# Two products on half of the rows each for the scores of a chunk's two heads, in place of one product padded with zeros

## The chip, the cores and the metric

The kernel runs on one core of a Trainium2 chip. A core has five engines that run side by side: TensorE (PE in the profile, with its weight loads as PEld), VectorE (DVE), ScalarE (ACT), GpSimd (POOL) and SyncE (SP, which issues DMAs). TensorE reads from the on-chip memory and writes to eight banks of accumulators (PSUM), 128 partitions by 512 float32 numbers each. The metric is the device time of one execution, in microseconds (us); less is better.

## The reference, cut to what matters

The program is a chain of three layers on 256 tokens of width 1024. The change is in the last mixer, in its recurrent branch: two directions (forward and backward), 16 heads of width 64, over 256 context tokens and then 256 tokens of the sequence. The recurrence is

```
def wkv_scan(s0, scan_in):
    def step(s, inp):
        w, kk, a, k, v, r = inp
        sa = jnp.einsum('dbhij,dbhj->dbhi', s, kk)
        s = s * w[..., None, :] - sa[..., :, None] * (kk * a)[..., None, :] + v[..., :, None] * k[..., None, :]
        return s, jnp.einsum('dbhij,dbhj->dbhi', s, r)
    return lax.scan(step, s0, scan_in)
```

The kernel computes it in chunks of 64 steps: eight chunks in each direction, four of the context and four of the sequence. Within a chunk it needs, for each head, the products of every step's vectors `kk*a` and `k` (scaled by decays) with every step's `kk` and, in the sequence's chunks, with every step's `r`, over the 64 channels of the head, masked to the steps that come before. These are the scores that the change is about.

## The kernel before, in words

The last mixer goes over eight pairs of heads (`i` from 0 to 7). For each pair there are four pieces of work: `rw_scores` (projections, decays, scores), `rw_inverse` (the inverse of a triangular matrix per chunk), `rw_chain` (the eight chunks one after the other) and `diff_head` (one head of the other branch, an attention). In one turn of the loop stand `chain(i)`, `inverse(i + 1)`, `heads(i + 1)` and `scores(i + 2)`, so four pairs are in work at a time. The order of the instructions on each engine is not the order of the code: the framework simulates the program when it is built and puts on each engine next what it takes to be ready. Each engine then works strictly through its own list.

A pair of heads takes 128 partitions: channels of the first head in partitions 0 to 63 and of the second in 64 to 127. In `rw_scores`, per direction `d`, `BK[:, c]` (L1682, L1685) holds for chunk `c` the 64 columns of `kk*a` and the 64 of `k` of both heads. `ap` (tiles `AL`, one of them in the space of `xT`) holds `kk` of the eight chunks and `r` of the last four, in a layout with an extra axis `o` for the head: L1679 and L1680 write head `o` on its own 64 partitions only, and the other 64 partitions of that column block are zeros, set once. So a product of `BK[:, c]` (128 weight columns) with `ap[:, c]` (128 columns: `o` by 64 steps) over all 128 partitions gives the scores of the two heads apart, in 128 rows.

The scores come in three tiles `mc` of PSUM per direction: at L1689 four products of 128 columns for the context's chunks; at L1696, twice, two products of 256 columns (`kk` and `r`) for two of the sequence's chunks each. VectorE multiplies them by a mask into `MA` and `MR`: L1690 once, L1699 four times. Then `BK` is transposed (L1703, tile `bt`). All of `rw_scores` (projections and `lo`, `la`, `kn`, `mc`, `bt`, `bo`, `gu`) draws its PSUM tiles from a pool of two banks, `a`, in turn (`self.banks(c2, a=2, i=1, r=2, d=2, k=1)`). `rw_chain` reads `MA` (L1743) and the zero-padded `AL` (L1747); `rw_inverse` reads `MA` (L1810 and on).

A float32 matmul stands in the trace as two passes, each a weight load and a matmul, so four products are eight rows there. Each row of the trace names the part of the array that it uses before the shape of the operand, as rows*columns: `128*128` is all of it, `64*128` one half of the rows.

Of the kernel before, what the change touches and what calls it, by code (L numbers as in the profile page):

```python
# [249 lines left out]
class K:  # L250
# [1351 lines left out]
    def rw_scores(self, i, h2):  # L1602

        nc, A = self.nc, self.A
        v_ = nc.vector
        g_ = nc.gpsimd
        p, tp = self.rp, self.rt
        lora = p.tile([128, 3, 128], F32, tag="lora", name=f"lora{i}", bufs=1)
        nc.sync.dma_start(lora, A["lora"][i])

        def proj(name, j, n):
            out = p.tile([128, n // T, T], F32, tag=name, name=f"{name}{i}", bufs=2 if name == "v" else 1)
            ps = self.psum(name, "k")
            self.wT(ps[:, :n], self.w2(24 + j), h2 if n > T else h2[:, :, T:])
            self.shift(ps[:, :n].rearrange("p (s t) -> p s t", t=T), j, out)
            return out

        lw = self.lw.rearrange("p s t -> p (s t)")
        c0 = math.exp(-0.5)

        def decays(d):

            pw, pa = self.psum("lo"), self.psum("la")
            nc.tensor.matmul(pw, lora[0:64, d], lw[0:64], start=True, stop=True)
            nc.tensor.matmul(pa, lora[64:128, d], lw[64:128], start=True, stop=True)
            t = tp.tile([128, 7, T], F32, tag="el", name=f"el{i}_{d}", bufs=1)
            sg, a, Pi = (t[:, 2 * m:2 * m + 2].rearrange("p s t -> p (s t)") for m in range(3))
            E3 = t[:, 6]
            nc.scalar.activation(sg, pw, AF.Tanh, bias=self.hb[:, 8 * d + i:8 * d + i + 1], scale=0.5)
            nc.scalar.activation(a, pa, AF.Tanh, bias=self.hb[:, 16 + 8 * d + i:17 + 8 * d + i], scale=0.5)  # L1630
            v_.tensor_scalar(t[:, 0:4], t[:, 0:4], 0.5, 0.5, op0=OP.mult, op1=OP.add)
            if d == 0:
                v_.tensor_tensor_scan(Pi, self.smask, sg, 0.0, op0=OP.mult, op1=OP.add)
            else:
                v_.tensor_tensor_scan(Pi[:, ::-1], self.smask, sg[:, ::-1], 0.0, op0=OP.mult, op1=OP.add)
            v_.tensor_sub(sg, Pi, sg)
            nc.scalar.activation(sg, sg, AF.Exp, scale=-c0)
            nc.scalar.activation(E3, Pi[:, T:], AF.Exp, scale=-c0)
            ends = Pi.rearrange("p (s c t) -> p s c t", s=2, t=64)
            nc.scalar.activation(WC[:, d].rearrange("p (s c) -> p s c", s=2), ends[:, :, ::-1, 0] if d else ends[:, :, :, 63], AF.Exp, scale=-c0)  # L1640
            nc.scalar.activation(Pi, Pi, AF.Exp, scale=c0)
            return sg, a, Pi, E3

        k = proj("k", 8 + i, 512)
        r = proj("r", i, T)

        kk = p.tile([128, 2, T], F32, tag="kk", name=f"kk{i}")
        sq = tp.tile([128, 2, T], F32, tag="sq", name=f"ksq{i}", bufs=1)
        v_.tensor_scalar(kk, k, self.pvec("rw_k_k", i), None, op0=OP.mult)
        nc.scalar.activation(sq, kk, AF.Square)  # L1650
        ps = self.psum("kn")
        nc.tensor.matmul(ps, self.bd, sq.rearrange("p j t -> p (j t)"), start=True, stop=True)
        rs = self.rstd(ps, 512, eps=self.lneps[:, 1:2])
        v_.tensor_mul(kk, kk, rs.rearrange("p (j t) -> p j t", j=2))

        AL = self.apart[i % 2]
        MA = p.tile([128, 2, 2, 8, 64], F32, tag="MA", name=f"MA{i}", bufs=2)
        MR = p.tile([128, 2, 2, 4, 64], F32, tag="MR", name=f"MR{i}", bufs=2)
        BKt = p.tile([128, 2, 7, 128], F32, tag="BKt", name=f"BKt{i}", bufs=2)
        WC = p.tile([128, 2, 8], F32, tag="WC", name=f"WC{i}", bufs=2)  # L1660
        for d in range(2):
            n = f"{i}_{d}"
            E1, a, E2, E3 = decays(d)
            t1 = E1

            def fl(x, s=None):
                x = x.rearrange("p (s t) -> p s t", t=T) if len(x.shape) == 2 else x
                if d:
                    x = x[:, :, ::-1]
                if s is None:  # L1670
                    return x.rearrange("p s (c t) -> p s c t", t=64)
                return x[:, s].rearrange("p (c t) -> p c t", t=64)

            BK = tp.tile([128, 8, 2, 64], F32, tag="BK", name="BK" + n, bufs=1)
            BK5 = BK.rearrange("p (s c) a t -> p s c a t", s=2)
            ap = AL[d]
            for o in range(2):
                rr = slice(64 * o, 64 * o + 64)
                v_.tensor_mul(ap[rr, :8, o].rearrange("p (s c) t -> p s c t", s=2), fl(kk)[rr], fl(E1)[rr])  # L1679
                v_.tensor_mul(ap[rr, 8:, o], fl(r, 0)[rr], fl(E3[:, None], 0)[rr])  # L1680
            v_.tensor_mul(t1, kk.rearrange("p s t -> p (s t)"), a)
            v_.tensor_mul(BK5[:, :, :, 0], fl(t1), fl(E2))  # L1682
            v_.tensor_scalar(a, a, self.pvec("rw_k_a", i), self.ka1[:, i:i + 1], op0=OP.mult, op1=OP.add)
            v_.tensor_mul(a, a, k.rearrange("p s t -> p (s t)"))
            v_.tensor_mul(BK5[:, :, ::-1, 1] if d else BK5[:, :, :, 1], *(x.rearrange("p (s c t) -> p s c t", s=2, t=64) for x in (a, E2)))  # L1685

            ps = self.psum("mc")
            for c in range(4):
                nc.tensor.matmul(ps[:, 128 * c:128 * c + 128], BK[:, c].rearrange("p a t -> p (a t)"), ap[:, c].rearrange("p o t -> p (o t)"), start=True, stop=True)  # L1689
            v_.tensor_mul(MA[:, d, :, 0:4].rearrange("p o c t -> p c o t"), ps.rearrange("p (c o t) -> p c o t", c=4, o=2),  # L1690
                          self.wmask[:, d, None, None, 0:64].to_broadcast([128, 4, 2, 64]))
            zz = ap.rearrange("p (m c) o t -> p m c (o t)", m=3)
            for c2 in range(2):
                ps = self.psum("mc")
                for c in range(2):
                    nc.tensor.matmul(ps[:, 256 * c:256 * c + 256], BK[:, 4 + 2 * c2 + c].rearrange("p a t -> p (a t)"), zz[:, 1:3, 2 * c2 + c], start=True, stop=True)  # L1696
                pv = ps.rearrange("p (c m o t) -> p m c o t", c=2, m=2, o=2)
                for m, dst in enumerate((MA[:, d, :, 4 + 2 * c2:6 + 2 * c2], MR[:, d, :, 2 * c2:2 * c2 + 2])):
                    v_.tensor_mul(dst.rearrange("p o c t -> p c o t"), pv[:, m], self.wmask[:, d, None, None, 64 * m:64 * m + 64].to_broadcast([128, 2, 2, 64]))  # L1699
            for s in range(2):  # L1700
                ps = self.psum("bt")
                for c in range(4 - s):
                    nc.tensor.transpose(ps[:, 128 * c:128 * c + 128], BK[:, 4 * s + c].rearrange("p a s -> p (a s)"), self.ident)  # L1703
                nc.scalar.copy(BKt[:, d, 4 * s:4 * s + 4 - s], ps.rearrange("p (c t) -> p c t", c=4)[:, :4 - s])
        v = proj("v", 16 + i, 512)

        sq = tp.tile([128, 2, T], F32, tag="sq", name=f"bsq{i}", bufs=1)
        v_.scalar_tensor_tensor(sq[:, 0], r[:, 0], self.pvec("r_k", i), k[:, 1], op0=OP.mult, op1=OP.mult)
        ps = self.psum("bo")
        nc.tensor.matmul(ps[:, :T], self.bd, sq[:, 0], start=True, stop=True)  # L1710
        bg = p.tile([128, 2, T], F32, tag="bg", name=f"bg{i}", bufs=2)
        v_.tensor_mul(bg[:, 0], v[:, 1], ps[:, :T])
        ps = self.psum("gu")
        nc.tensor.matmul(ps[:, :T], lora[:, 2], self.sgd[:, 0], start=True, stop=True)
        nc.scalar.copy(bg[:, 1], ps[:, :T])
        return v, AL, MA, MR, BKt, WC, bg
# [523 lines left out]
```

## Time and profile before

| | |
|---|---|
| median of 3 runs | 3490.37 us (3477.37 to 3495.87) |
| profiled execution | 3489.14 us |
| its span, first to last instruction | 3487.4 us |
| TensorE busy over the span | 92% |
| VectorE busy over the span | 66% |
| mean granted TensorE clock | 0.936 of full |
| stretch that holds all the scores of the mixer | 1600 to 2440 us of the span |

A busy TensorE is not TensorE at its peak: matmuls follow each other before the one ahead has ended, so the price of one in a row of equals is the distance from start to start, not its duration. The granted clock is given as a share of 2.4 GHz: it stands at 1.2 or at 2.4 GHz, and a number between is a mean over a stretch.

### The profile page before, as it was taken

What the parts mean: (1) busy time and instruction counts of PE and PEld (TensorE: products, weight loads), DVE (VectorE), ACT (ScalarE), POOL (GpSimd) and SP (SyncE); (2) the same over time, 40 slices, a digit from 0 to 9 for tenths busy, and PEclk for the clock granted to TensorE, in tenths of its full rate; (3) what the DMA queues carried; (4) which work ended last, traced back from release to release, by engine and by line L of the source; (5) the groups of instructions that cost most, each with busy time, mean ns of one, the idle gap of its engine ahead of it and who ended that gap; (6) DMA issues with size and microseconds to landing.
All of it is one profiled execution on the core that took longest, in us unless ns stands there. A gap on an engine that the chain in (4) does not pass through costs nothing. (4 is left out here: it accounts for less than half of the span.)

```text
span 3487.4 us, 67773 instructions
## 1 busy us (share of the span) xinstructions
PE 3207.4 (92%) x26800; PEld 2648.6 (76%) x26800; DVE 2309.6 (66%) x4717; ACT 1710.9 (49%) x3107; POOL 467.2 (13%) x478
## 2 busy tenths in 40 slices
PE   6989979989999999978899999899879989999999
PEld 4869967766668888746677677667779989988888
DVE  3568858753449999746766666566357767756665
ACT  4445423442226666514544544454436658755554
POOL 0000232200000000010000000000208853410000
PEclk8999988889999999988989888889789999999999
DMA  7666574478798999962111111111435545566775
GB/s 291 237 225 229 200 255 147 125 282 319 321 372 327 337 338 339 356 264 78 45 31 45 45 45 40 45 44 47 141 123 191 159 141 173 176 197 202 231 228 163
DMA packets 162435, 658.51 MB, mean 189 GB/s; under 512 B 18216, under 2 KB 37304, under 8 KB 118208
## 3 DMA queue, kind: packets, MB, share of 16 engines
q1 hardware_dynamic: 145344, 572.33, 46.6%
q0 software_dynamic: 16768, 81.80, 6.9%
q8 instruction: 212, 3.47, 0.4%
q14 instruction: 111, 0.91, 0.1%
HBM read 634.26 MB, written 19.79 MB: 188 GB/s over the span
## 5 line engine op out<-in xcount | busy, mean ns | idle before, releaser
L428 PE MATMUL mg<-mg,xs 128*64 128x256 f32 x1408 | 185.0, 386 | 3.7 <-ACT xf L1101 3.7
L1248 ACT ACTIVATE msg<-mg 128x128 f32<-128x128 f32 (+1 forms) x154 | 42.1, 273 | 260.3 <-PE mg L428 191.2
L428 PEld LDWEIGHTS mg<-mg,xs 128*64 128x64 f32 x1408 | 106.2, 138 | 68.1 <-issue 15.8
L331 PE MATMUL mod<-wm,c 128*32 128x256 f32 x1152 | 100.2, 452 | 50.0 <-DMA wm<-mods 45.5
L1363 POOL DMA_DIRECT2D h2h<-hch x1 | 1.0, 960 | 821.6 <-DVE squares L1372 821.6
L331 PEld LDWEIGHTS mod<-wm,c 128*32 128x32 f32 x1152 | 37.7, 123 | 87.7 <-DMA wm<-mods 44.4
L1814 POOL MEMSET X<- 128x272 f32 x8 | 3.0, 378 | 753.6 <-DVE UV L1754 217.9
L1249 DVE TENSOR_TENSOR msg<-msg,mg 128x128 f32<-128x128 f32 (+1 forms) x154 | 43.4, 282 | 76.4 <-ACT msg L1248 75.9
L328 POOL DMA_DIRECT2D wm<-mods x64 | 34.6, 541 | 386.2 <-PE mod L331 374.5
L2024 POOL TENSOR_SCALAR oh<-iota,idx 128x128 f32<-128x128 f32 x44 | 58.3, 1324 | 146.1 <-PE G L2034 146.1
L2027 ACT ACTIVATE oh<-oh,idx 128x128 f32<-128x128 f32 x212 | 69.1, 393 | 6.4 <-DVE oh L2019 6.4
L2019 DVE TENSOR_TENSOR oh<-iota,idx 128x1024 f32<-128x1024 f32 x53 | 67.6, 1278 | 0.0
L2034 PE MATMUL G<-oh 128*128 128x128 f32 x512 | 62.5, 275 | 0.0
L1152 DVE COPY mgt<-mg 128x128 f32<-128x128 f32 x44 | 12.8, 290 | 75.0 <-PE mg L1145 74.8
L367 DVE RECIPROCAL rs<-rs 128x512 f32<-128x512 f32 (+1 forms) x16 | 44.0, 2752 | 27.7 <-ACT rs L366 27.6
L2034 PEld LDWEIGHTS G<-oh 128*128 128x128 f32 x512 | 60.1, 192 | 0.0
L428 PE MATMUL ya<-md,mgt 128*64 128x512 f32 x176 | 55.1, 604 | 4.2 <-DVE mgt L1152 4.0
L2067 POOL DMA_DIRECT2D a<-ad x32 | 17.3, 542 | 284.9 <-DVE ap48l L446 127.1
L428 PE MATMUL yb<-md,mgt 128*64 128x512 f32 x176 | 54.0, 592 | 0.0
L2039 ACT COPY Gate<-G 128x288 f32<-128x288 f32 x64 | 43.3, 678 | 20.4 <-DVE acts L2038 20.4
L1760 PEld LDWEIGHTS S<-UV,BKt 128*64 128x64 f32 x448 | 22.3, 150 | 37.3 <-issue 13.8
L928 PE MATMUL y<-st,s5c 128*32 128x128 f32 x256 | 43.7, 320 | 6.5 <-DVE st L920 6.5
(11890 smaller groups left out, 12677.0 us busy)
## 6 DMA issues: line engine op xcount, KB each, us to landing
mg<-m_gu SPq DMA_DIRECT2D x176, 1024.0 KB, 7.8
md<-m_dn SPq DMA_DIRECT2D x88, 1024.0 KB, 8.0
wm<-mods POOLq DMA_DIRECT2D x64, 1024.0 KB, 6.1
w<-u SPq DMA_DIRECT2D x128, 512.0 KB, 3.7
w<-v SPq DMA_DIRECT2D x128, 512.0 KB, 4.2
w<-w_in SPq DMA_DIRECT2D x132, 256.0 KB, 2.7
w<-e_gu SPq DMA_DIRECT2D x44, 512.0 KB, 4.4
w<-e_in SPq DMA_DIRECT2D x24, 512.0 KB, 4.8
```

Source lines behind the costliest of these rows:

```text
L328: (nc.gpsimd if later else nc.sync).dma_start(ws, self.A["mods"][g, kp].rearrange("p j k c -> p (j k) c"))
L331: nc.tensor.matmul(ps[32 * j:32 * j + 32, :256], c[:, 2 * kp + k, :], ws[:, 2 * j + k, :], start=kp + k == 0, stop=kp + k == 4)
L367: nc.vector.reciprocal(t[:, :n], t[:, :n])
L428: mm(ps, w, h, start=start, stop=stop, **kw)
L928: nc.tensor.matmul(py[o, 128 * j:128 * j + 128], self.s5c[:, ci + m, i0 + r], st[:, r, m, off:off + 128], start=False, stop=m == 1, skip_g ...
L1248: nc.scalar.activation(sg[:rows], ps[:rows, :128], AF.Silu)
L1249: v.tensor_mul(sg[:rows], sg[:rows], ps[:rows, 128:256])
L2019: v_.tensor_tensor(o, iota.rearrange("p (a b i) -> p a b i", a=1, b=1).to_broadcast([128, 2, 4, 128]), idx[:, 0:2, 4 * t4:4 * t4 + 4].rear ...
L2024: nc.gpsimd.tensor_scalar(o[:, 0, t], iota, i1, w, op0=OP.is_equal, op1=OP.mult)
L2027: nc.scalar.activation(o[:, 0, t], o[:, 0, t], AF.Copy, scale=w)
L2034: nc.tensor.matmul(ps[:, 128 * t:128 * t + 128], o[:, 1, t], o[:, 0, t], start=True, stop=True)
L2039: nc.scalar.copy(G[0][:, :, ts].rearrange("p i t -> p t i"), pv[:, :, HF:120])
```

## The change

Each product over 128 partitions with zeros in half of the moving operand becomes two products over 64 partitions, one for each head (`o`): the weights are `BK`'s 64 rows of that head, the moving columns the head's own. The scores of head 0 go to one bank and those of head 1 to another. So there are eight products of 64 columns in place of four of 128, and eight of 128 columns in place of four of 256. The tiles `mc` are two pairs per direction where there were three single ones. VectorE's multiplies are six of 128x256 in place of one of 128x512 and four of 128x256. `ap` keeps its zeros, which `rw_chain` still needs.

```
--- before.py
+++ after.py
@@ -1684,19 +1684,22 @@
-            ps = self.psum("mc")
+            zz = ap.rearrange("p (m c) o t -> p m c o t", m=3)
+            hh = [slice(0, 64), slice(64, 128)]
+            ps = [self.psum("mc") for o in range(2)]
             for c in range(4):
-                nc.tensor.matmul(ps[:, 128 * c:128 * c + 128], BK[:, c].rearrange("p a t -> p (a t)"), ap[:, c].rearrange("p o t -> p (o t)"), start=True, stop=True)
-            v_.tensor_mul(MA[:, d, :, 0:4].rearrange("p o c t -> p c o t"), ps.rearrange("p (c o t) -> p c o t", c=4, o=2),
-                          self.wmask[:, d, None, None, 0:64].to_broadcast([128, 4, 2, 64]))
-            zz = ap.rearrange("p (m c) o t -> p m c (o t)", m=3)
-            for c2 in range(2):
-                ps = self.psum("mc")
-                for c in range(2):
-                    nc.tensor.matmul(ps[:, 256 * c:256 * c + 256], BK[:, 4 + 2 * c2 + c].rearrange("p a t -> p (a t)"), zz[:, 1:3, 2 * c2 + c], start=True, stop=True)
-                pv = ps.rearrange("p (c m o t) -> p m c o t", c=2, m=2, o=2)
-                for m, dst in enumerate((MA[:, d, :, 4 + 2 * c2:6 + 2 * c2], MR[:, d, :, 2 * c2:2 * c2 + 2])):
-                    v_.tensor_mul(dst.rearrange("p o c t -> p c o t"), pv[:, m], self.wmask[:, d, None, None, 64 * m:64 * m + 64].to_broadcast([128, 2, 2, 64]))
+                for o in range(2):
+                    nc.tensor.matmul(ps[o][:, 64 * c:64 * c + 64], BK[hh[o], c].rearrange("p a t -> p (a t)"), zz[hh[o], 0, c, o], start=True, stop=True)
+            for o in range(2):
+                v_.tensor_mul(MA[:, d, o, 0:4], ps[o][:, :256].rearrange("p (c t) -> p c t", c=4), self.wmask[:, d, None, 0:64].to_broadcast([128, 4, 64]))
+            ps = [self.psum("mc") for o in range(2)]
+            for c in range(4):
+                for o in range(2):
+                    nc.tensor.matmul(ps[o][:, 128 * c:128 * c + 128], BK[hh[o], 4 + c].rearrange("p a t -> p (a t)"), zz[hh[o], 1:3, c, o], start=True, stop=True)
+            for o in range(2):
+                pv = ps[o].rearrange("p (c m t) -> p m c t", c=4, m=2)
+                for m, to in enumerate((MA[:, d, o, 4:8], MR[:, d, o])):
+                    v_.tensor_mul(to, pv[:, m], self.wmask[:, d, None, 64 * m:64 * m + 64].to_broadcast([128, 4, 64]))
```

The lines behind the edit move down by three (L1703 becomes L1706). The scheduler also puts much else of the mixer in a slightly different order.

On TensorE, the scores of the last pair of heads in the second direction stand so before. A number behind a name tells tiles of one name apart: `mc_24945` is the tile of the context's chunks, `mc_24951` and `mc_24956` are those of the sequence's.

```order
L1689 MATMUL mc_24945<-AL_16722,BK_1_24935 128x128 x4
L1696 MATMUL mc_24951<-AL_16722,BK_1_24935 128x256 x2
L422 MATMUL v_25855<-h2l,w23600h 128x512
L423 MATMUL v_25855<-h2h,w23600l 128x512
L1760 MATMUL S_25125<-UV_25103,BKt_23674 64x64 x4
L1743 MATMUL R_25133<-UV_25103,MA_23672 64x64 x4
L1696 MATMUL mc_24956<-AL_16722,BK_1_24935 128x256 x2
L1703 MATMUL bt_24961<-c_ident,BK_1_24935 128x128 x4
```

The same place on TensorE now. `mc_25095` and `mc_25107` are the banks of head 0, `mc_25096` and `mc_25108` those of head 1; the left out lines repeat the two ahead of them, eight in all.

```order
L1692 MATMUL mc_25095<-AL_16722,BK_1_25085 128x64
L1692 MATMUL mc_25096<-AL_16722,BK_1_25085 128x64
...
L1755 MATMUL U_25303<-R_1_25292,TT_24404 64x64 x4
L1509 MATMUL v_26054<-c_ident,dvc_26052 128x128 x4
L1519 MATMUL ds_26062<-dk_25912,dq_25963 128x512
L1698 MATMUL mc_25107<-AL_16722,BK_1_25085 128x128 x4
L1698 MATMUL mc_25108<-AL_16722,BK_1_25085 128x128 x4
L1763 MATMUL S_25310<-UV_25263,BKt_23794 64x64 x4
L1746 MATMUL R_25319<-UV_25263,MA_23792 64x64 x4
```

The products of the first set alternate between the heads. Those of the second set stand four of head 0 and then four of head 1, and the scheduler has moved this set as a whole to behind other work, where half of it stood right behind the first set before. In ten of the sixteen blocks (eight pairs, two directions) the second set stands so, four and four.

In the other six the second set alternates. The first of the second direction of pair 1, on TensorE, before:

```order
L1689 MATMUL mc_17861<-AL_16722,BK_1_17851 128x128 x4
L1696 MATMUL mc_17867<-AL_16722,BK_1_17851 128x256 x2
L421 MATMUL v_18691<-h2h,w17540h 128x512
...
L1887 MATMUL p_17333<-TT_17180,P_17227 16x16 x64
L1696 MATMUL mc_17872<-AL_16722,BK_1_17851 128x256 x2
L1703 MATMUL bt_17877<-c_ident,BK_1_17851 128x128 x4
```

And there now, from the second set on (the left out lines are six more, in turn):

```order
L1890 MATMUL p_17353<-TT_17200,P_17247 16x16 x64
L1698 MATMUL mc_17903<-AL_16722,BK_1_17881 128x128
L1698 MATMUL mc_17904<-AL_16722,BK_1_17881 128x128
...
L423 MATMUL v_18731<-h2h,w17580l 128x512
L421 MATMUL r_18886<-h2h,w17730h 128x256
```

Here eight products of 128 columns in turn stand where two of 256 columns stood, and the transposes that followed at once (L1703) now come later.

## Rows read from the trace of the kernel before

**Rows 1.** The page: its first line, and the engines' busy time (share of the span, instructions).

```profile
span 3487.4 us, 67773 instructions
PE 3207.4 (92%) x26800; PEld 2648.6 (76%) x26800; DVE 2309.6 (66%) x4717; ACT 1710.9 (49%) x3107; POOL 467.2 (13%) x478
```

**Rows 2.** Busy time by stretch: PE, PEld, DVE, ACT, POOL (instructions); clock, DMA share, GB/s.

```profile
1600.00:2440.00 840.00, 769.50 (x8738) 592.63 (x8737) 550.88 (x1172) 391.99 (x713) 4.05 (x14) 0.88 0.15 44
```

**Rows 3.** The same in two short stretches of the mixer.

```profile
2000.00:2050.00 50.00, 49.29 (x654) 40.09 (x655) 30.82 (x57) 21.09 (x38) 0.00 (x0) 0.73 0.13 37
...
2400.00:2450.00 50.00, 46.60 (x506) 37.09 (x505) 31.43 (x82) 21.55 (x44) 0.00 (x0) 1.00 0.19 57
```

**Rows 4.** The same stretch, instructions on tile mc alone: PE, PEld, DVE, clock, DMA.

```profile
1600.00:2440.00 840.00, 60.33 (x256) 43.56 (x256) 34.88 (x80) 0.88 0.15 44
```

**Rows 5.** Timeline of PE: start, duration, line, tiles, rows*columns of the array, shape, passes.

```profile
1713.77 2.09 PE L1879 MATMUL p<-P,TT 32*32 32x16 f32 x64
1715.79 1.16 PE L1689 MATMUL mc<-AL,BK 128*128 128x128 f32 x8
1716.79 1.03 PE L1696 MATMUL mc<-AL,BK 128*128 128x256 f32 x4
...
1720.87 1.69 PE L1887 MATMUL p<-TT,P 32*16 32x16 f32 x128
1722.49 1.13 PE L1696 MATMUL mc<-AL,BK 128*128 128x256 f32 x4
1723.46 0.60 PE L1703 MATMUL bt<-c_ident,BK 128*128 128x128 f32 x4
```

**Rows 6.** Timeline of PE: products of two halves of the rows, two banks.

```profile
1742.13 0.69 PE L1519 MATMUL ds<-dk,dq 64*128 64x512 f32 x1
1742.15 0.69 PE L1625 MATMUL la<-lw,lora 64*128 64x512 f32 x1
1742.67 0.59 PE L1519 MATMUL ds<-dk,dq 64*128 64x512 f32 x1
1742.68 0.59 PE L1625 MATMUL la<-lw,lora 64*128 64x512 f32 x1
1743.10 1.02 PE L1624 MATMUL lo<-lw,lora 64*128 64x512 f32 x2
```

**Rows 7.** Timeline of PE: into another tile size and back.

```profile
1755.70 0.28 PE L423 MATMUL gz<-h2h,w17940l 128*128 128x256 f32 x1
1755.82 0.28 PE L421 MATMUL gz<-h2h,w17940h 128*128 128x256 f32 x1
1756.03 0.27 PE L1747 MATMUL R<-S,xT 128*64 128x64 f32 x1
...
1756.20 0.22 PE L1747 MATMUL R<-S,xT 128*64 128x64 f32 x1
1756.20 0.22 PE L1747 MATMUL R<-S,AL 128*64 128x64 f32 x1
1756.26 0.22 PE L1747 MATMUL R<-S,xT 128*64 128x64 f32 x1
...
1756.41 0.39 PE L422 MATMUL gz<-h2l,w17940h 128*128 128x256 f32 x1
1756.64 0.28 PE L423 MATMUL gz<-h2h,w17940l 128*128 128x256 f32 x1
```

**Rows 8.** Timeline of PE: many weight columns, few moving columns.

```profile
1698.99 2.05 PE L1858 MATMUL tc<-r_eye,pad 128*64 128x32 f32 x32
```

**Rows 9.** Groups on DVE by line and shape: busy us, mean ns, idle before.

```profile
L1699 DVE TENSOR_TENSOR MA<-mc,r_wmask 128x256 f32<-128x256 f32 x32 | 13.5, 422 | 7.3 <-PE mc L1696 7.1
L1690 DVE TENSOR_TENSOR MA<-mc,r_wmask 128x512 f32<-128x512 f32 x16 | 11.0, 688 | 10.1 <-PE mc L1689 10.1
```

**Rows 10.** Who waited for whom, PE, 1600 to 2440: us, times, longest.

```profile
PE mc L1696 <- DVE MA L1690: 3.1, 1, 3.1
```

## Prediction

> **What bounds the kernel now.** I read the busy shares first, then busy time by stretch, then the instructions on the tile that the change touches, then timelines for the price of one pass, last the waits. TensorE is the engine to look at: it is busy 92% of the span, VectorE 66% [rows 1]. In the stretch from 1600 to 2440 us, which holds all of the scores, it is 769.5 of 840 us, again 92%, with VectorE at 551 us [rows 2]. So a microsecond taken from TensorE there should come back nearly whole, and one added should cost the same; VectorE has room. The second thing to see is the clock: 0.88 over the stretch, that is, about 24% of it at 1.2 GHz [rows 2]. Third, how small the object is: everything that TensorE does on the tile mc is 60.3 us, overlaps at the ends included [rows 4], 1.7% of the span. Even half of it is only 30 us.
>
> **The price of a pass.** Each float32 product is two passes. At full clock the eight passes of 128 columns at L1689 stand 1.00 us ahead of L1696; 0.1 us of that belongs to the change of tile size from the line before (priced below), so a pass takes about 0.11 us. The four passes of 256 columns before L1703 take 0.97 us, with the same 0.1 us in it, so 0.215 us each [rows 5]. The column count sets it there. But where weights are many and moving columns few, the weights set it: L1858 has 64 weight columns and only 32 moving, and its 32 passes take (2.05 − 0.22)/31 = 0.059 us each [rows 8], the same 0.06 us as L1747, with 64 and 64 [rows 7]. Hence a pass with 128 weight columns should not go under about 0.11 us, however few columns move.
>
> **First set of products (context's chunks).** Before: 8 passes of 128 columns, 8 × 0.11 = 0.88 us. Now: 16 passes of 64 columns with 128 weight columns each, in turn on the two halves of the rows. The trace has such a pair: `ds` and `la`, each on 64 rows and with a bank of its own, start 0.02 us apart, and their second passes 0.01 us apart; both together, four passes, are done when `lo` starts, 0.97 us after [rows 6]. Serially, at the 0.43 us from the second passes to `lo`, four passes would take 1.7 us. So halves of the rows do run side by side. The new set then is 8 pairs at the weight price, 8 × 0.11 = 0.88 us: nothing won, nothing lost.
>
> **Second set (sequence's chunks).** Before: 8 passes of 256 columns, 1.72 us a block, 16 blocks. Now 16 passes of 128 columns. Where the heads alternate, 8 pairs, 0.88 us: 0.84 us won, in 6 blocks, −5.0 us. In ten blocks the order has four of head 0 and then four of head 1, in TensorE's own list. The nearest rows are L1879 and L1887. L1879's products go sixteen on one group of rows, then sixteen on another: (2.09 − 0.18)/63 = 0.030 us a pass. L1887's alternate: (1.69 − 0.17)/127 = 0.012 us a pass, two to two and a half times as fast [rows 5]. They differ in weight columns too (32 and 16), so this is no pure test, but it says that neighbours in the list run together and distant ones don't. Four and four would be 16 × 0.11 = 1.76 us: nothing won. The bounds for the ten are 0 and, if head 1's products overtook, −8.4 us; I take a quarter, −2 us, for the overlap where the two fours meet.
>
> **Changes of tile size.** The products move from 128\*128 to 64\*128, between neighbours of every size. Going from `gz` to `R`, the distance is 0.21 us in place of 0.12: 0.09 us added. Going back, `gz` starts 0.15 us after the last `R` pass in place of 0.06 and its second matmul comes 0.23 us later in place of 0.12: 0.2 us added, the weights no longer loaded in advance [rows 7]. So a change costs 0.09 to 0.2 us, 0.15 in the middle. I gave each line in the two orders the tile size that the trace prints for it and 64\*128 to the new products: between the first scores and the last chain there are 728 places where neighbours differ before and 774 now, 46 more. 46 × 0.15 = +6.9 us (4.1 to 9.2).
> The Trainium skill ("TensorEngine Tiling (Array Packing)", Key Properties) says that a change of tiling mode, not just of tile, drains TensorE. By that rule, with which the 0.09 us and 0.2 us agree, the tiling's "2×" for a contraction of 64 is not free for short bursts such as these.
>
> **VectorE.** Six multiplies of 128x256 at 0.422 us are 2.53 us a block; before it was 0.688 + 4 × 0.422 = 2.38 us [rows 9]. That is +0.15 × 16 = 2.5 us on an engine that is idle a third of the stretch: hidden, at most +2.5 us.
>
> **Banks.** The pool has two. Before, the first half of the second set went into the second bank while VectorE emptied the first. Now both banks hold the first set, and the second set must wait for both multiplies, 0.84 us. The scheduler has put other work there (attention, chain, inverse), so I cost it at nothing. If VectorE comes late this cover is gone; the one such wait of before, L1696 on L1690, was 3.1 us [rows 10]. Bounds: 0, and 3.1 us in about six blocks, +19 us.
>
> **The sum.** −5.0 − 2 + 6.9 = −0.1 us at full clock, and the same at 0.88. From the profiled execution's 3489.1 us (span 3487.4 and 1.7 around it) that is 3489; the median of the runs shown is 3490.4, 1.3 above. I predict 3490 us.
>
> **Rivals.**
> *Full overlap.* Head 1's four overtake head 0's: −5.0 − 8.4 + 4.1 = −9.3, over 0.88 −10.6: 3479 us. For it, the pair `ds`, `la`; against it, L1879.
> *Twofold everywhere.* By the speed of 2 both sets would halve: 16 × (0.44 + 0.86) = −21 us, +6.9 for the changes, over 0.88 −16: 3473 us. Against it, L1858's price by weights. (The same page's Overview gives "up to 2×" for small contractions; no row here shows it for 64 moving columns on 128 weight columns.)
> *Slower by the banks.* The second set waits at the head of TensorE's list for VectorE's two multiplies; behind it in the list stand `bt`, the chain's `S` and `R`, and everything else. 3.1 us in six blocks, +19 us: 3508 us. It decides once VectorE takes the first-set multiplies over some 2 us late. For it: the multiplies are two in a row now and VectorE's queue holds 0.7 us casts and long reciprocals. Against it: the waits on mc are few now.
> *The pair doesn't overlap at all.* The second set gains nothing, the first set doubles (+0.88 × 16 = 14 us), +6.9: +21, over 0.88 +24: 3513 us. Against it, rows 6.
> *The clock shifts.* A stretch of 50 us with TensorE busy 49.3 us had 0.73, one with 46.6 us had 1.00 [rows 3]: work that stands elsewhere can meet another clock. A mean of 0.86 or 0.90 in place of 0.88 is ±0.02/0.88 × 770 = ±17 us: 3473 or 3507. For it, that much of the mixer's order moves; against it, sixteen such stretches average out.
>
> **How the numbers follow.** Forecast 0.52; full overlap 0.10; twofold 0.05; banks 0.13; no overlap 0.04; clock 0.16, half each way. A measurement tells about 0.5% from no change, 17.5 us, so 3473 to 3508. Faster: half of the twofold (0.03), half of the faster clock (0.04), tails of the rest with the runs' own spread of ±9 us (0.08): 0.15. Slower: half of the banks (0.07), no overlap (0.03), half of the slower clock (0.04), tails (0.04): 0.18. Same: 0.67. The likeliest case alone spans 3479 to 3501: bounds of the overlap, of the changes and of VectorE, and the runs' spread. The range takes in full overlap, most of the clock and the banks' end: 3469 to 3511.
>
> **What would show it.** The new rows at L1692 in pairs a few hundredths apart, 0.11 us from pair to pair; L1698 the same where heads alternate, serial where they stand four and four; TensorE on mc falling only from 60 us to about 50 to 55; about 0.1 us ahead of each set. Wrong if L1698's fours run side by side, if pairs at L1692 come at 0.06 us, if the waits of L1692 and L1698 on VectorE add up to over 10 us, or if the mean clock of the mixer moves by over 0.02.

## The result, and the profile after

The changed kernel takes 3535.35 us (median of 4 runs, 3526.78 to 3544.69) against 3490.36 (4 runs, 3477.37 to 3495.87): 1.0137 of the time before, 95% interval 1.0106 to 1.0169. It is 45 us slower, outside the range of 3469 to 3511.

The page of the changed kernel, with the same lines as [rows 1]:

```profile
span 3524.8 us, 68297 instructions
...
PE 3241.8 (92%) x27056; PEld 2677.9 (76%) x27056; DVE 2311.7 (66%) x4733; ACT 1708.3 (48%) x3105; POOL 466.6 (13%) x478
```

TensorE is busy 34 us longer, VectorE as long as before. Where: busy time of the engines (PE, PEld, DVE, ACT, POOL), granted clock, DMA share and GB/s from the first product on `mc` to the last of `bt`; before in the first fence, after in the second, whose last line is the tile `mc` alone (answering to [rows 2] and [rows 4]).

```profile
1610.80:2416.20 805.40, 741.57 (x8444) 571.84 (x8445) 523.75 (x1113) 375.54 (x680) 4.05 (x14) 0.88 0.14 43
```

```profile
1614.90:2455.60 840.70, 764.40 (x8722) 590.24 (x8722) 527.51 (x1134) 375.71 (x683) 3.25 (x14) 0.85 0.13 41
...
1614.90:2455.60 840.70, 50.83 (x512) 44.44 (x512) 35.30 (x96) 0.85 0.13 41
```

The stretch is 35.3 us longer, nearly all that the two profiled executions differ by (37.4). The scores themselves did become cheaper, 60.3 to 50.8 us. TensorE's idle time in the stretch rose by 12.5 us (63.8 to 76.3), and all that is not the scores is busy 32 us longer, though its instructions are the same but for a few at the ends. The granted clock fits this: 0.88 became 0.85. The clock records of the two profiles, added up over the stretch, are 189 us at 1.2 GHz before and 256 now; 67 us more at half speed cost TensorE up to 33 us. The timeline of TensorE after (start, duration, line, tiles, rows*columns, shape, passes) shows it on an ordinary projection:

```profile
1644.76 1.31 PE L1692 MATMUL mc<-AL,BK 64*128 64x64 f32 x16 [2.80 <-DVE BK L1685]
...
1648.42 0.41 PE L421 MATMUL r<-h2h,w16760h 128*128 128x256 f32 x1
1648.63 0.41 PE L422 MATMUL r<-h2l,w16760h 128*128 128x256 f32 x1
...
1649.49 0.28 PE L422 MATMUL r<-h2l,w16770h 128*128 128x256 f32 x1
1649.61 0.28 PE L423 MATMUL r<-h2h,w16770l 128*128 128x256 f32 x1
...
1650.04 1.16 PE L1698 MATMUL mc<-AL,BK 64*128 64x128 f32 x16
...
2096.54 3.09 PE L1698 MATMUL mc<-AL,BK 64*128 64x128 f32 x16
2099.43 1.91 PE L1519 MATMUL ds<-dk,dq 64*128 64x512 f32 x2
```

The same 256 columns start 0.21 us apart at 1648 us, behind a first set, and 0.12 apart a microsecond later. A second set whose heads alternate takes 1.16 us at 1650; one that stands four and four takes 3.09 us at 2096, at 1.2 GHz, and what follows it is still slow.

### The profile page after: what moved, and what is told of

It reads as the page before. It is cut to its first block, busy times and chain, and to the rows that moved or that the text cites. A ratio compares the mean times of both kernels' runs of the same rounds, so it can differ in the third digit from the quotient of the medians.

```text
span 3524.8 us, 68297 instructions
## 1 busy us (share of the span) xinstructions
PE 3241.8 (92%) x27056; PEld 2677.9 (76%) x27056; DVE 2311.7 (66%) x4733; ACT 1708.3 (48%) x3105; POOL 466.6 (13%) x478
## 4 chain that ended last, share of the span: by engine, by line
PE 44%; DVE 6%; ACT 3%; issue 1%; DMA 1%; POOL 0%; DVEq 0%; ACTq 0%; SPq 0%; POOLq 0%
PE acc L421 3%; PE acc L422 3%; PE acc L423 3%; PE act L423 3%; PE act L421 3%; PE act L422 3%; PE G L2037 2%; PE qk L421 1%; PE qk L422 1%; PE qk L423 1%; PE ds L1519 1%; PE v L421 1%; PE v L422 1%; PE v L423 1%; PE R L1746 1%
## 5 line engine op out<-in xcount | busy, mean ns | idle before, releaser
L331 PEld LDWEIGHTS mod<-wm,c 128*32 128x32 f32 x1152 | 37.4, 122 | 88.9 <-DMA wm<-mods 45.9
L1763 PE MATMUL S<-UV,BKt 128*64 128x64 f32 x448 | 37.8, 264 | 15.9 <-ACT UV L1756 11.1
```

What stands on the lines that cost most here:

```text
L331: nc.tensor.matmul(ps[32 * j:32 * j + 32, :256], c[:, 2 * kp + k, :], ws[:, 2 * j + k, :], start=kp + k == 0, stop=kp + k == 4)
```

## The experiments

The whole run's time at 1.2 GHz can be had for every run, traced or not: 2 x (1 - granted clock) x span. Below are its mean over the runs, and the same from the clock records of the traced stretch (first `mc` to last `bt`). The runs of the kernel before scatter between some 395 and 490 us by the first measure, so a difference of 10 us in a mean says little; its mean was 442 to 445 in every set. By the second measure there is one trace of each kernel. The rows *before* and *e9* are the same instructions in the same order, and their stretches differ by 7 us, and by 17 us at 1.2 GHz, so smaller differences between two traces say nothing.

| kernel | median us | ratio, 95% interval | at 1.2 GHz, run | stretch us | at 1.2 GHz, stretch |
|---|---|---|---|---|---|
| before | 3490 | | 443 | 805 | 189 |
| after | 3535.35 | 1.0106-1.0169 | 562 | 841 | 256 |
| e1 new products, old order | 3536.06 | 1.0094-1.0183 | 527 | 845 | 273 |
| e2 old products, new order | 3508.52 | 1.0043-1.0083 | 474 | 815 | 188 |
| e3 half rows, old order | 3530.0 | 1.0091-1.0188 | 526 | 837 | 256 |
| e4 pair, all rows, old order | 3534.68 | 1.0106-1.0202 | 498 | 846 | 216 |
| e6 tile change only | 3515.94 | 1.0053-1.0102 | 469 | 829 | 201 |
| e7 half rows, first set | 3498.57 | 1.0013-1.0058 | 459 | 804 | 179 |
| e8 half rows, second set | 3520.68 | 1.0073-1.0133 | 505 | 841 | 260 |
| e9 before, order written out | 3489.29 | 0.9984-1.0021 | 445 | 798 | 172 |
| e10 after + 4 full products | 3534.14 | 1.0087-1.0141 | 525 | 860 | 266 |
| e11 before + 4 full products | 3500.65 | 1.0014-1.0049 | 442 | 812 | 175 |
| e13 after + whole sets | 3532.71 | 1.0089-1.0180 | 484 | 847 | 206 |
| e14 pairs in first set only | 3511.97 | 1.0054-1.0113 | 510 | 823 | 209 |

In the old order means: the instructions of TensorE, VectorE and ScalarE in the last mixer follow a table of the order that the kernel before has.

```
+        for e, table in ORDER.items():
+            ...
+            for a, b in zip(at, at[1:]):
+                tc.add_manual_dep(mine[b], mine[a].name, ...)
```

**e1 and e2: products or order?** e1 is the edit with that table; e2 is the kernel before with the table of the changed kernel's order.

> The changed products, multiplies and banks, with the order of everything else on TensorE, VectorE and ScalarE pinned to what it was before; the products of both sets alternate between the heads in all 16 blocks. If the loss of 45 us comes from the new order that the scheduler made (theory O), this one is at the old time or a little below: the scores on TensorE fall from 60 us to about 47, changes of tile size give some 5 to 9 us back: 3478 to 3492 us, mean clock of the stretch with the scores 0.88. If the products on half of the rows themselves let the clock fall or the pair of banks makes TensorE wait (theory T), it stays slow, 3515 to 3540 us, clock about 0.85.

> The products, multiplies and banks of before, with the order of everything else pinned to what the scheduler made for the changed kernel. Theory O: slow, 3520 to 3540 us, and a clock of about 0.85 in the stretch. Theory T: back at 3485 to 3500 us with a clock of about 0.88.

e1: 1.0139, as slow as the changed kernel, without its order. e2: 1.0063, half of it, and its stretch has no more time at 1.2 GHz than before. So the order costs 23 us by the medians, of which the traced stretch shows 9, with more pauses (77 us idle against 64), and the products make the clock fall without the new order. In the old order the banks do cost. The waits of e1 (engine, tile, line, what for; us, times, longest):

```profile
PE bt L1706 <- DVE MR L1702: 23.3, 15, 4.2
PE mc L1692 <- DVE BK L1685: 7.2, 3, 3.8
PE mc L1698 <- DVE MA L1694: 3.6, 2, 3.4
```

`bt` stood right behind the scores and now waits until VectorE has emptied both banks. The scheduler's new order moves it away: in the changed kernel the same wait is 1.8 us.

**e3 and e4: rows or banks?** e3 has no pair and no second bank; e4 has both, but no half rows.

```
-... BK[:, c].rearrange("p a t -> p (a t)"), ap[:, c].rearrange("p o t -> p (o t)"), ...
+... BK[0:64, c].rearrange("p a t -> p (a t)"), ap[0:64, c].rearrange("p o t -> p (o t)"), ...   # e3, and alike in the second set
+... BK[:, c].rearrange("p a t -> p (a t)"), zz[:, 0, c, o], ...                                 # e4, o = 0 and 1 in a bank each
```

> The kernel before in its exact order, but each product of the scores reads only the lower 64 rows of both operands, so the scores of the upper head are left out: same number of products, passes, banks and multiplies, only the tile size on the array is 64*128. It prices the tile size alone. Theory O: the 46 or so added changes of tile size, 4 to 9 us: 3494 to 3500 us, clock 0.88. Theory T, if the clock follows the rows in use: 3515 us or more and a clock under 0.87.

> As the first of these (two banks, one for each head, new multiplies, old order of the rest), but each of the 16 products of a block reads all 128 rows, zeros included, so nothing runs side by side and the tile size stays 128*128. The first set costs 16 passes of 0.11 us where 8 stood, +0.88 us in 16 blocks = +14 us; the second 16 of 0.11 in place of 8 of 0.215, about +1. Theory O: 3500 to 3508 us. Theory T by the banks: the waits of TensorE on the multiplies come on top, 3515 us or more; by the rows in use: 3500 to 3508 us.

e3 is the clearest run of the study: as many instructions, in the same order, on the same columns, waiting no longer (59 us idle in the stretch against 64), and 1.0139. Its whole runs have 84 us more at 1.2 GHz than the kernel before; at half speed that is 42 of the 44 us that it is slower. It leaves out the upper head's scores, so the work behind them has other numbers in it; e1, whose numbers are right, loses as much of the clock (273 us in the stretch). At one place, TensorE before and in e3:

```profile
1821.61 1.91 PE L1696 MATMUL mc<-xT,BK 128*128 128x256 f32 x4
...
1825.66 1.13 PE L1696 MATMUL mc<-xT,BK 128*128 128x256 f32 x4
...
1830.51 1.12 PE L1624 MATMUL lo<-lw,lora 64*128 64x512 f32 x2
```

```profile
1843.54 1.91 PE L1696 MATMUL mc<-xT,BK 64*128 64x256 f32 x4
...
1849.22 2.07 PE L1696 MATMUL mc<-xT,BK 64*128 64x256 f32 x4
...
1858.19 2.07 PE L1624 MATMUL lo<-lw,lora 64*128 64x512 f32 x2
```

Both enter this block at 1.2 GHz, behind the small products `p`. Before, the scores on all rows are followed by full clock; on half of the rows they are not, and TensorE stays at 1.2 GHz for 37.5 us. The same 34 us by windows, before and in e3, 0.87 and 0.51:

```profile
1821.60:1855.50 33.90, 29.33 (x326) 21.95 (x324) 21.88 (x49) 16.13 (x32) 0.00 (x0) 0.87 0.04 13
```

```profile
1841.60:1875.80 34.20, 31.08 (x177) 20.86 (x178) 18.79 (x39) 12.35 (x23) 0.00 (x0) 0.51 0.02 5
```

e4 is as slow as e1, but in part of other things: its scores take 79 us in place of e1's 44, its clock falls less (216 against 273 us in the stretch). It still falls, though all products are on all rows: 498 us in the whole runs against 442.

**e6: is it the changes of tile size?** One product on 64 rows ahead of each group of scores, overwritten by it.

```
+            nc.tensor.matmul(ps[:, 0:64], BK[0:64, 0].rearrange("p a t -> p (a t)"), ap[0:64, 0, 0], ...)
```

> The kernel before in its own order, with one product more of 64 columns on 64 rows ahead of each of the 48 groups of scores (its result is overwritten by the group): the same changes of tile size as with products on half of the rows, but the scores themselves stay on all rows. Its own price: 48 x 2 passes of 0.11 us = 10.6 us, and one to two changes of 0.09 to 0.2 us at each, 48 to 96 x 0.15 = 7 to 14 us: about 3506 us from 3485.6. Theory 1 (rows in use): 3500 to 3512, and some 190 to 205 us of the mixer's stretch at 1.2 GHz, as before (189). Theory 2 (changes of tile size): the clock falls as it did with the half rows in the old order, 256 us at 1.2 GHz, and the time is 3506 + 33 = 3539.

3516, between the two. In the stretch the work on `mc` grew by 27.3 us for 48 products, 0.57 each, of which some 0.22 are its two passes: an estimate of 0.35 for the changes of tile size, in and out. The time at 1.2 GHz grew by 12 us in the stretch, less than *before* and *e9* differ by, against 67 in e3; over the whole runs it grew by 27 us, against 84. So the changes explain a third of the fall at most.

**e7 and e8: which set?** As e3, in one set alone.

> The kernel before in its own order; only the first set (context's chunks) reads the lower 64 rows, so the upper head's scores of these chunks are left out. With both sets it was 3530, 44 us over before. Theory 1 (rows in use, by the passes' columns): the first set holds a third of the columns, so about a third of it, +15: 3500. Theory 2 (changes of tile size): one group of three in a block, +15 too. If the clock falls by single events of which either set suffices: 3515 to 3530.

> The kernel before in its own order; only the second set (sequence's chunks) reads the lower 64 rows, so the upper head's scores of these chunks are left out. Theory 1 (rows in use, by the passes' columns): two thirds of the 44 us, +29: 3515, with some 230 us of the stretch at 1.2 GHz. Theory 2: two groups of three, the same. The two parts add up to the 44 us if stretches at 1.2 GHz come each from its own set; if they come from single events, the sum of the two is over 55 us or under 35.

Of the 44 us, the second set alone costs 35 and the first 12, whose stretch shows nothing of it. e9 puts that size in place: the kernel before with its own order written out.

> The kernel before with its own order of TensorE, VectorE and ScalarE in the last mixer written out as a table, as in the runs in the old order, and nothing else. It says what a difference between two medians is worth: the run with half rows in the first set was 12 us over before although its stretch of the mixer was 1 us shorter. If that is the spread of the rest of the program: ratio 1.000 within 0.003, 3476 to 3496 us. If writing out the order costs something by itself: some 10 us over, 3496, and the other runs in the old order are to be read against this one.

The table costs nothing (1.0003). The 12 us of e7 are then more than scatter by its interval, but where they arise its trace, of its fastest run, doesn't show. Over the whole runs it has 17 us more at 1.2 GHz, which would be some 8 of the 12.

**e5 and e12: the clock by itself.**

> A kernel of its own: it leaves out the whole computation and runs float32 products of 128 columns on TensorE in stretches, each behind 160 products on all 128 rows. Stretches of one kind: all rows; all rows with zeros in half of the moving operand; pairs on the two halves of the rows; one half of the rows alone; products of 32 rows and 16 columns. Then eight of each kind in turn with eight on all rows, eight in turn with 64 of the small ones, and eight with a pause behind them. Theory 1 (the rows in use): all rows and zeros keep a granted clock of 1.00 in the dense stretches; one half alone falls to 0.5 to 0.7 although TensorE is never idle; pairs lie between; behind the small products the sets on all rows keep a higher clock than the sets on one half, by 0.05 or more. Theory 2 (changes of tile size, which empty TensorE for a moment, and the idle time that they make): the dense stretches all keep 1.00, halves and pairs too, since no tile size changes in them, and only the stretches in turn fall. Theory 3 (the zeros): the zeros alone have another clock than all rows.

> A kernel of its own again, without the computation: 30 times 64 small products and behind them a set, for eight kinds of set, then 30 times 16 pairs of products of 64 rows and 64 columns and behind them a set, for three kinds. From the first such kernel: eight on all rows 0.95, eight pairs on the two halves 0.73, eight on one half 0.53. If a pair counts for less than a product on all rows but not for nothing: sixteen pairs come near eight on all rows, 0.90 or more; four on all rows behind eight pairs 0.90 or more too, behind eight on one half 0.75 or more. If what counts is the tile size and not the rows: products on all rows with half of the weight columns in turn (128x64) give 0.73 as the pairs do; if it is the rows, they give 0.95. Behind the pairs of 64x64, which are on half of the rows themselves, the same order of the kinds, and less apart.

Each of the two was run once. Windows of e5: PE, PEld, DVE, POOL, clock, DMA, GB/s. The small products have 32 rows and 16 columns. First pairs on the two halves, dense, one half, dense, and the small products alone; then, with 64 small products in turn: eight on all rows, the same with zeros, eight pairs, eight on one half.

```profile
276.20:356.60 80.40, 80.40 (x1440) 80.35 (x1440) 0.00 (x0) 0.00 (x0) 1.00 0.01 2
392.80:473.20 80.40, 80.40 (x721) 80.40 (x720) 0.00 (x0) 0.00 (x0) 1.00 0.01 1
509.30:598.80 89.50, 45.93 (x3201) 43.48 (x3200) 0.00 (x0) 0.00 (x0) 0.53 0.02 4
...
1141.90:1242.30 100.40, 83.94 (x3456) 78.03 (x3456) 0.00 (x0) 0.00 (x0) 0.95 0.02 4
1278.20:1380.70 102.50, 85.27 (x3458) 79.29 (x3457) 0.00 (x0) 0.00 (x0) 0.93 0.02 4
1416.60:1536.20 119.60, 105.35 (x3839) 98.30 (x3840) 0.00 (x0) 0.00 (x0) 0.73 0.02 4
1572.30:1703.60 131.30, 129.01 (x3457) 122.89 (x3456) 0.42 (x1) 0.00 (x0) 0.53 0.01 3
```

Dense products on half of the rows keep 1.00, against what theory 1 said. Among small products it is as it said: with the same number of changes of tile size, sets on all rows keep 0.95, zeros or not, pairs 0.73, one half 0.53. (The stretches with a pause tell nothing: the scheduler put other products into the pauses.) e12, behind 64 small products each: eight on all rows, four on all rows, eight pairs, sixteen pairs, eight pairs and four on all rows, eight on one half and four on all rows, and eight times two products on all rows that take half of the weight columns each (128\*64).

```profile
43.50:173.60 130.10, 110.92 (x4324) 103.02 (x4323) 0.00 (x0) 0.00 (x0) 0.90 0.02 4
209.20:325.40 116.20, 113.45 (x4083) 105.57 (x4082) 0.00 (x0) 0.00 (x0) 0.52 0.02 4
361.70:508.60 146.90, 128.24 (x4803) 119.63 (x4801) 0.00 (x0) 0.00 (x0) 0.76 0.02 4
544.40:710.30 165.90, 154.56 (x5763) 146.40 (x5761) 0.00 (x0) 0.00 (x0) 1.00 0.02 4
746.00:897.60 151.60, 136.29 (x5044) 125.37 (x5044) 0.00 (x0) 0.00 (x0) 0.97 0.02 4
...
1135.20:1344.30 209.10, 208.50 (x4563) 195.04 (x4562) 0.00 (x0) 0.00 (x0) 0.56 0.01 3
1381.40:1521.60 140.20, 113.01 (x4804) 102.06 (x4802) 0.43 (x1) 0.00 (x0) 0.88 0.02 4
```

The second line matters most: half as many products on all rows, 0.52 in place of 0.90. In this mixture, taking out work on all rows is enough to lose the clock. Sixteen pairs (1.00) and four full products behind eight pairs (0.97) keep it, as expected. Two expectations fell: four full products behind eight on one half don't bring it back (0.56, not 0.75), and sets behind pairs of 64x64 are all at 1.00. Products on all rows with half of the weight columns (last line, 0.88) come near those with all of them, not near the pairs. The busy share of the profile doesn't go with it: 98% busy at 0.53, 84% at 0.95 (e5's last line and the one for eight on all rows). The Trainium skill ("TensorE: Matmul & The Clock Gate", Part 1) says that the clock is set by how busy TensorE has been recently. These two lines go against it if busy is read as the share that the profile counts.

**e10, e11, e13: the work put back.** Four products of 128 columns on all rows ahead of each second set, overwritten by it, in the changed kernel (e10) and in the kernel before (e11); four of 256, the whole old second set, in the changed kernel (e13).

```
+            for c in range(4):
+                nc.tensor.matmul(ps[c // 2][:, 256 * (c % 2):256 * (c % 2) + 256], BK[:, 4 + c]..., zf[:, 1:3, c], ...)   # e13
```

> The changed kernel in its own order, with four products of 128 columns on all 128 rows ahead of each of the 16 second sets (the set overwrites their results). Work added at full clock: 16 x 8 passes x 0.11 = 14 us. Theory 1 (products on half of the rows let the clock stay low behind small products; products on all rows bring it back, as in the kernel that ran the clock by itself): the time at 1.2 GHz falls from 256 us to 190 to 215, which gives 20 to 33 us back: 3535 + 14 - 27 = 3522, less than the changed kernel although TensorE does more. Theory 2 (the clock falls with the tile sizes' drains or the pauses of the new order, not with the rows): no change of the clock, 3549.

> The kernel before in its own order with the same four products on all rows ahead of each second set (overwritten). The other half of the pair: theory 1 says that little is to be had where the sets stand on all rows already: 14 us of work and 0 to 10 us back by the clock, 3490 to 3500, with 170 to 190 us of the stretch at 1.2 GHz. If products on all rows help the clock wherever they stand, as much as in the changed kernel: 3486 + 14 - 27 = 3473, and that would be a kernel faster than both.

> The changed kernel in its own order, with the whole second set of the kernel before (four products of 256 columns on all rows, overwritten by the pairs) ahead of each of the 16 second sets: twice what the run with full products added. Work added at full clock: 16 x 8 x 0.215 = 27.5 us. Theory 1 (it is the work on all rows that was taken out; half of it did not end the long low period at 2092 us, where the old products of 3.78 us did): the stretch's time at 1.2 GHz comes back from 256 us to 175 to 205, and the time is 3535 + 27.5 - 33 = 3530, with no more than 14 us at 1.2 GHz at a time. Theory 2 (something else of the pairs holds the clock down, such as their drains): 250 us or more at 1.2 GHz as in the changed kernel, and 3563.

e10 came out between its two theories, 3522 and 3549: 3534, and its stretch is at 1.2 GHz as long as the changed kernel's (266 and 256 us). Over the whole runs it has 37 us less there, so by that measure half of the products brought back a part. e13 came out as theory 1 said: 3532.71, with 206 us at 1.2 GHz in place of 256 in the stretch and 484 in place of 562 in the whole runs. Only its periods at 1.2 GHz are longer than expected: two last 17 and 20 us, where 14 was to be the most. The place that the timeline after shows at 2096 us, in e2, e10 and e13:

```profile
2102.08 3.78 PE L1696 MATMUL mc<-AL,BK 128*128 128x256 f32 x8
2105.79 1.14 PE L1519 MATMUL ds<-dk,dq 64*128 64x512 f32 x2
```

```profile
2102.39 2.08 PE L1697 MATMUL mc<-AL,BK 128*128 128x128 f32 x8
2104.40 3.09 PE L1700 MATMUL mc<-AL,BK 64*128 64x128 f32 x16
2107.29 1.91 PE L1519 MATMUL ds<-dk,dq 64*128 64x512 f32 x2
```

```profile
2097.94 3.17 PE L1698 MATMUL mc<-AL,BK 128*128 128x256 f32 x8
2101.05 1.71 PE L1701 MATMUL mc<-AL,BK 64*128 64x128 f32 x16
2102.59 1.02 PE L1519 MATMUL ds<-dk,dq 64*128 64x512 f32 x2
```

At this one place, behind the whole old set `ds` takes 1.0 to 1.1 us, behind half of it and the pairs 1.9. With all of it, some 30 us of work whose results are thrown away (TensorE on `mc` 81.3 us in place of 50.8), the changed kernel takes no longer than without; in the kernel before, half as much work added cost 11.5 us.

**e14: the pairs in the first set alone**, in the changed kernel's order.

> The changed kernel's order, with the pairs of products in the first set alone; the second set is the one of the kernel before, on all rows. With the old products in both sets this order took 3508, with the pairs in both 3535. Theory 1 with the second set as what counts (half rows in the first set alone cost 12 us in the old order, in the second 35): 3508 to 3515, and 180 to 205 us of the stretch at 1.2 GHz. If the first set counts as much as the second: 3520 or more, and 220 us or more.

3512, within 4 us of e2, and 209 us, a little over what was expected. So in the new order too it is mostly the second set: 23 us of its 27 by the medians. The time at 1.2 GHz over the whole runs gives the first set a larger part: 474 us in e2, 510 here, 562 after.

None of the versions beats the kernel before.

## Why the prediction was wrong

- **TensorE bounds the stretch**: right. What was missed is that its speed there hangs on what it works on.
- **First set, nothing won**: right. At full clock products of 64 columns start 0.112 us from pair to pair (L1692, blocks that nothing interrupts), and in e5 720 products in pairs take the 80.4 us of 360 on all rows.
- **Second set**: right. At full clock, from the first start to the last, 0.89 us where the heads alternate and 1.44 where they stand four and four, near the 0.88 and the 1.76 less 0.2 of the sum; `mc` fell to 50.8 us, within the 50 to 55.
- **Changes of tile size, 0.15 us**: in e5 eight pairs in turn with eight on all rows take 94.9 us and all on all rows 85.6: 9.3 us for 48 changes, 0.19 each, the upper part of 0.09 to 0.2.
- **VectorE**: hidden, as said; its busy time over the span is the same (2309.6 and 2311.7 us).
- **Banks**: *slower by the banks* isn't what happened: the second set waited 0.7 us in all. In the old order it would have: e1's `bt` waits 23 us. The new order has other waits instead; idle time rose by 12.5 us, where 0 was put in. That is the smaller step that failed.
- **"The sum −0.1 at full clock, and the same at 0.88"** is the step that failed. The clock was taken from the stretch before as a given, as if it didn't hang on what the change does to the products; it fell to 0.85. Of the 35 us of the stretch 32 are other work made longer, which the fall accounts for, 12.5 the pauses, and the scores give 9.5 back. The prediction's own sign of being wrong, a mean clock that moves by over 0.02, is the one that came. The rival *the clock shifts* named the place, but for a wrong reason (work that stands elsewhere, of either sign, averaging out over sixteen blocks) and with half of the size; e3 shows the fall with nothing moved. [rows 3] gave a hint: there the busier stretch has the lower clock.
- **The sum at full clock** came out, in part by luck. Take all work at 1.2 GHz as twice as long as at full clock (an estimate): the traced stretch less half of its time at 1.2 GHz is 711 us before, 712 in e9, 709 in e3, 711 in e8, 713 after and 720 in e2. So nothing but the clock separates e3 and e8 from the kernel before, and without the clock the change is worth about nothing. But the sum had nothing for the order, which costs some 9 us by e2, and its products with their changes of tile size, put at nothing together, win some 7. (Over whole runs the same estimate gives 3254.5 us after and 3266.3 before. In the two profiled executions that gain lies outside the stretch, which holds all the changed products, so it isn't shown to come from the change.)

Left open: why e2's whole runs have 31 us more at 1.2 GHz while its traced stretch has none (in its trace the surplus stands mostly ahead of the stretch, 204 us against 166, where the traces of all these kernels range from 146 to 204), and why e4's clock fell at all. A trace is one execution, and the pauses that both have weren't tried by themselves. That work on all rows among small products decides the clock is shown by e3, e8, e12 and e13; by what measure the chip weighs it is not.

## What to carry to other kernels

Zeros in an operand are not free work to be taken out where TensorE is near the lower clock: price the change at the clock that is left, not at the one that the profile shows. Where a stretch mixes small products with a few on all rows, those few can hold the clock for all that stands around them, as the second set does here, so look at what runs at full speed right behind them before halving them. To tell a clock effect from an order effect, write the old order out and change the operands alone.

## What was not expected of the hardware

Adding some 30 us of useless products to the changed kernel cost nothing measurable (3535.35 and 3532.71). Zeros in half of the moving operand made hardly a difference to the clock (0.93 and 0.95, one stretch each), nor did half of the rows as long as nothing smaller stood in between (1.00). Eight products on one half among small ones left the clock where the small ones alone have it (0.53 in both).
